# Grouped-query attention on one core: the first head's loads and turns in another order, the last head's output scaled and stored in another way

## The chip, the cores and the metric

The kernel runs on one core of a Trainium2 chip. The metric is device time in microseconds for one execution; lower is better. Each kernel was run several times, and the median is given with the lowest and the highest.

## The reference

```python
batch, n_q_heads, n_kv_heads, seq, head_dim = (8, 8, 2, 1024, 64)     # float32 q, k, v
...
scale = 1.0 / np.sqrt(head_dim)
for g in range(n_kv_heads):
    q_group, k_group, v_group = ...                                    # 4 q heads, 1 k head, 1 v head
    scores = scale * np.matmul(q_group, k_group.transpose(0, 1, 3, 2))
    attn = np.exp(scores - scores.max(-1))
    attn = attn / (attn.sum(-1) + 1e-08)
    output[:, heads of g] = np.matmul(attn, v_group)
```

There are 64 heads of q (8 batches of 8), each with 1024 queries and 1024 keys of length 64. Four heads of q share one head of k and v.

## The kernel before, in words

One head of q is a job; there are 64 jobs, j = 0 to 63. The scores of a job are computed transposed, keys on partitions: 8 pieces of 128 keys by 1024 queries. q and k lie in SBUF as bf16, transposed, with two rows of the sequence side by side, so that the 64 elements of the even rows lie on partitions 0 to 63 and those of the odd rows on 64 to 127. One score is a pair of matmuls (L735), one on each half of the partitions, into a PSUM tile of 128 x 1024 (two banks). There are three such tiles, sp0 to sp2, called slots.

A score is turned into exponentials in one of two ways. ScalarE (ACT) takes 382 of the 512 scores with its Exp function (L747). VectorE (DVE) takes the other 130 with an integer approximation: a pass out of PSUM (L758), then four passes in SBUF over two scores at once (L765, L772, L781, and L786 in the last two jobs). The results are the weights of the second product (L799), whose moving operand is v with a column of ones, so that the sum of the exponentials comes out as column 65. Its output goes to two more PSUM banks. VectorE takes reciprocals of the sums (L852), scales up to seven output pieces at a time into SBUF (L855), and SP stores a whole head (L870).

The order of the work on each engine is fixed when the kernel is built. A planner (class Plan) simulates PE, ACT and DVE with costs in nanoseconds and writes a list of events; M_START is the time at which it lets the first score start. Loads and casts are hung on this list at fixed distances before a job's first score: the cast of q to bf16 in DRAM 18 us before (POOL's queue, cast_q, L527), its transposing load 11 us before (SP's queue, turn_q, L570). Engines then wait for each other by semaphores alone.

The first job doesn't wait for that route. Its q and k are loaded as float32 (L589, L590): k's first chunk of 128 pairs of keys and then the other three on SP's queue, all of q on ACT's. While they are on their way, PE multiplies blanks (dummy, L600), eight of 512 columns. VectorE casts k's first chunk and q's second half to bf16 (L605, L607), ACT casts q's first half and the rest of k (L606, L608). PE turns the four chunks of q and then the four of k with an identity matrix (turn, L614): q into one slot, k's first chunk into another, the rest of k into the third. Then ACT copies columns 0 to 319 of the turned q to SBUF (L624), VectorE k's first chunk (L625), q's columns 320 to 511 (L626) and the rest of k (L627). The first score needs all of q and k's first chunk. Behind it PE computes k's other arrangement, even and odd rows swapped (swap_k0, L633), which VectorE copies (L637), and the remaining scores follow. The second score goes to VectorE, the third to ACT as its second exp. In gaps of this early stretch the planner puts more blanks of 128 columns.

The last job's second product is written to a free slot (L820), half of the eight output pieces in each bank, as soon as the last exps end. VectorE takes all eight reciprocals (L852), then scales the first four pieces (L855), and ACT the other four, one instruction each (L863). The two halves are stored separately (L831), the first on SP's queue and the second on ACT's. Each half is 128 partitions by two runs of 512 bytes; one partition's rows of the output lie 256 rows apart.

In what the traces print, q, k are tiles of the first job in float32 or bf16, qd and kd the casts in DRAM, qt and kt the transposed tiles, sp the slots, ops the two output banks, pt the results of ACT's exps, yt, zt and et VectorE's, and ost the ring of outputs in SBUF.

Of the kernel before, what the change touches and what calls it, by code (L numbers as in the profile page):

```python
# [8 lines left out]


M_START = 5800
M_SWAP = 1500
M_Q1 = 3400
M_QSTEP = 2700
# [11 lines left out]
M_FIX = 66  # L26
M_DTAIL = 80
M_DEP = 34
M_D1 = 1.042
# [18 lines left out]
PB = 7  # L48
NPIECE = 8
# [62 lines left out]
class Plan:  # L112
# [79 lines left out]
    def dve(self, s):  # L192
        t, nj, end = s.tD, self.nj, None
        if s.dq and s.dq[0][0] <= t:
            _, sl, j, c = s.dq.pop(0)
            n = len(STEPS) if j >= nj - TAIL else 3
            if s.open and s.open.nsteps != n:
                s.chains.append(s.open)
                s.open = None
            if s.open is None:  # L200
                s.open = Chain(s.nch, n)
                s.heads[s.nch] = []
                s.nch += 1
                s.used_c += 1
            ch = s.open
            ch.pairs.append((j, c))
            if j not in s.heads[ch.id]:
                s.heads[ch.id].append(j)
            self.gpsimd(s, t, j)
            s.note(t, "dpass", sl, (ch.id, len(ch.pairs) - 1), (j, c))  # L210
            end = t + M_FIX + 1024 * M_D1
            s.slot[sl] = end + M_DTAIL + M_SEE
            s.dlast = (ch.id, 0)
            if len(ch.pairs) == 2:
                s.chains.append(ch)
                s.open = None
        elif s.norms and s.norms[0][0] <= t and s.norms[0][1] == "rec":
            _, _, lo, hi = s.norms[0]
            s.note(t, "rec", (lo, hi), None, None)
            end = t + M_REC  # L220
            s.dlast = lo
            s.norms[0] = (end, "norm", lo, hi)
        else:
            best = None
            if s.norms and s.norms[0][0] <= t:
                late = s.dlast == s.norms[0][2]
                best = (late, 5 if late else 0, None)
# [224 lines left out]
def kernel(  # L452
# [158 lines left out]
    turned = {"k": new_slot(2)[:, 0, :], "q": new_slot(1)[:, 0, :], "k0": new_slot(0)[:, 0, :]}  # L611

    def turn(x, c):
        nc.tensor.matmul(  # L614
            turned["k0" if x == "k" and c == 0 else x][:, c * 128 : (c + 1) * 128],
            lhsT=b16[x][:, c, :], rhs=ident, start=True, stop=True,
        )

    for c in range(NH):
        turn("q", c)  # L620
    for c in range(NH):
        turn("k", c)
    QS = 320
    nc.scalar.activation(out=q0[:, 0, 0:QS], in_=turned["q"][:, 0:QS], func=AF.Copy)  # L624
    nc.vector.tensor_copy(out=k0[:, 0, 0:128], in_=turned["k0"][:, 0:128])  # L625
    nc.vector.tensor_copy(out=q0[:, 0, QS:HS], in_=turned["q"][:, QS:HS])  # L626
# [69 lines left out]
    for when, kind, x, j, c, *cols in ev:  # L696
# [30 lines left out]
        elif kind == "score":  # L727
# [4 lines left out]
            for half in range(2):  # L732
# [7 lines left out]
                    stop=True,  # L740
                )
            if len(where_s) == 1:
                swap_k0()
        elif kind == "act":
            p = pp.tile([128, 2, HS], BF16, name="pt")
# [81 lines left out]
                    )  # L827
        elif kind == "half":
            b, h = divmod(NJ - 1, H)
            r = plan.last % RING + x * 4  # L830
            (nc.scalar if x else nc.sync).dma_start(  # L831
                out=rows(out[b, h])[:, 2 * x : 2 * x + 2],
                in_=ost[:, r : r + 4, :].rearrange("p (s two) d -> p s (two d)", two=2),
            )
        elif kind in ("rec", "norm"):
            lo, hi = x
# [2 lines left out]
            if lo < plan.last:  # L839
                o = ops[plan.group_of[lo] % 2][:, 0 : n * (D + 1)]  # L840
                o = o.rearrange("p (s d) -> p s d", d=D + 1)
                sums = o[:, :, D]
            else:
                o2 = sps[plan.spare][:, :, 0 : 4 * (D + 1)]
                o2 = o2.rearrange("p b (s d) -> p b s d", d=D + 1)
                o, sums = o2[:, 0], o2[:, :, :, D]
            if kind == "rec":
                rec = rp.tile([128, NPIECE], FP32, name="rec")
                to = rec[:, 0:n]
                if lo >= plan.last:  # L850
                    to = to.rearrange("p (b s) -> p b s", b=2)
                vec = nc.vector.reciprocal(out=to, in_=sums)  # L852
            else:
                n = min(n, PB if lo < plan.last else 4)
                vec = nc.vector.tensor_tensor(  # L855
                    out=ost[:, r : r + n, :],
                    in0=o[:, :, 0:D],
                    in1=rec[:, 0:n].unsqueeze(2).to_broadcast([128, n, D]),
                    op=ALU.mult,
                )  # L860
                if lo >= plan.last:
                    for i in range(4):
                        nc.scalar.activation(  # L863
                            out=ost[:, r + 4 + i, :], in_=o2[:, 1, i, 0:D],
                            func=AF.Copy, scale=rec[:, 4 + i : 5 + i],
                        )
        elif kind == "store":
            b, h = divmod(j, H)
            r = j * NPIECE % RING
# [35 lines left out]
```

The softmax here doesn't subtract the row's maximum and nothing guards it: scores larger than these inputs give would overflow.

## Time and profile before

| | |
|---|---|
| Median of 5 runs | 364.87 us (364.27 to 365.48) |
| The profiled execution's own time | 364.27 us |
| Its span, first to last instruction | 362.5 us |
| Busy: PE, DVE, ACT, POOL | 96%, 97%, 98%, 14% |
| First score, first exp | 6.13 us, 6.56 us |
| End of the last second product, last store issued | 357.5 us, 359.27 us |

PE is TensorE's matmul row, PEld its weight loads, which overlap matmuls. DVE is VectorE, ACT is ScalarE, POOL is GpSimd, SP the engine that only issues DMAs; a q behind a name (SPq) stands for an engine's sequencer, which waits and issues. A number behind L is a line of the kernel. Times of a timeline or chain are microseconds from the span's start: the start, then the duration.

### The profile page before, as it was taken

What the parts mean: (1) busy time and instruction counts of PE and PEld (TensorE: products, weight loads), DVE (VectorE), ACT (ScalarE), POOL (GpSimd) and SP (SyncE); (2) the same over time, 40 slices, a digit from 0 to 9 for tenths busy, and PEclk for the clock granted to TensorE, in tenths of its full rate; (3) what the DMA queues carried; (4) which work ended last, traced back from release to release, by engine and by line L of the source; (5) the groups of instructions that cost most, each with busy time, mean ns of one, the idle gap of its engine ahead of it and who ended that gap; (6) DMA issues with size and microseconds to landing.
All of it is one profiled execution on the core that took longest, in us unless ns stands there. A gap on an engine that the chain in (4) does not pass through costs nothing.

```text
span 362.5 us, 13853 instructions
## 1 busy us (share of the span) xinstructions
PE 347.2 (96%) x6179; PEld 222.1 (61%) x6179; DVE 350.2 (97%) x481; ACT 354.1 (98%) x390; POOL 50.8 (14%) x100
## 2 busy tenths in 40 slices
PE   8879999999999999999999999999999999999993
PEld 3436666666666666666666666666666666656563
DVE  4999999999999999999999999999999999999992
ACT  5999999999999999999999999999999999999995
POOL 3121111111111111110111211111112101110000
PEclk9999999999999999999999999999999999999999
DMA  6635789377766874696576687768668776763223
GB/s 158 119 72 98 140 136 175 74 156 138 123 129 111 166 137 97 138 141 140 75 145 136 132 147 117 150 132 148 115 119 128 153 132 105 160 134 62 60 60 89
DMA packets 89307, 44.81 MB, mean 124 GB/s; under 512 B 45504, under 2 KB 87616, under 8 KB 88000
## 3 DMA queue, kind: packets, MB, share of 16 engines
q1 hardware_dynamic: 86336, 33.31, 41.3%
q0 software_dynamic: 2496, 10.23, 22.8%
q8 instruction: 48, 0.79, 0.9%
q10 hardware_dynamic: 416, 0.39, 0.4%
q14 instruction: 11, 0.09, 0.1%
HBM read 25.17 MB, written 27.00 MB: 144 GB/s over the span
## 4 chain that ended last, share of the span: by engine, by line
ACT 95%; PE 3%; issue 1%; DVE 0%
ACT pt L747 95%; PE ops L600 1%; PE sp L820 1%; PE sp L735 0%; PE ops L799 0%; ACT ost L863 0%; ACT qt L624 0%; PE sp L614 0%; DVE qt L626 0%; DVE warm L519 0%
## 5 line engine op out<-in xcount | busy, mean ns | idle before, releaser
L747 ACT ACTIVATE pt<-sp 128x1024 bf16<-128x1024 f32 x382 | 350.5, 1067 | 0.9 <-PE sp L735 0.9
L735 PE MATMUL sp<-qt,kt 64*128 64x512 bf16 x1024 | 173.9, 382 | 8.6 <-ACT pt L747 4.7
L799 PE MATMUL ops<-va,pt 128*128 128x65 bf16 x3008 | 181.7, 194 | 0.0
L799 PEld LDWEIGHTS <-pt 128*128 128x128 bf16 x3008 | 139.8, 98 | 34.1 <-issue 34.1
L758 DVE TENSOR_SCALAR yt<-sp 128x1024 uint16<-128x1024 f32 x130 | 158.1, 1216 | 0.3 <-PE sp L735 0.2
L799 PE MATMUL ops<-va,zt 128*128 128x65 bf16 x1024 | 136.0, 194 | 0.0
L799 PE MATMUL ops<-va,et 128*128 128x65 bf16 x1008 | 133.0, 195 | 0.0
L799 PEld LDWEIGHTS <-et 128*128 128x128 bf16 x1008 | 85.7, 98 | 30.4 <-issue 29.8
L799 PEld LDWEIGHTS <-zt 128*128 128x128 bf16 x1024 | 88.4, 98 | 7.5 <-issue 7.5
L735 PEld LDWEIGHTS <-kt 64*128 64x128 bf16 x1024 | 48.1, 93 | 57.1 <-issue 35.2
L781 DVE TENSOR_TENSOR zt<-yt,zt 128x2048 bf16<-128x2048 bf16 x65 | 78.2, 1204 | 0.0
L527 POOL DMA_DIRECT2D qd<-in_q_dram x63 | 32.5, 516 | 187.8 <-PE sp L735 176.7
L855 DVE TENSOR_TENSOR ost<-ops,rec 128x448 f32<-128x448 f32 x72 | 44.2, 614 | 0.0
L765 DVE TENSOR_SCALAR zt<-yt 128x2048 uint16<-128x2048 uint16 x65 | 44.0, 677 | 0.2
L772 DVE TENSOR_SCALAR et<-yt 128x2048 uint16<-128x2048 uint16 x65 | 43.3, 666 | 0.0
L535 POOL DMA_DIRECT2D kd<-in_k_dram x15 | 7.9, 525 | 51.5 <-PE sp L735 51.5
L552 POOL CAST va<-vs 128x512 bf16<-128x512 f32 x16 | 9.9, 617 | 36.6 <-DVE zt L781 16.4
L852 DVE RECIPROCAL rec<-ops 128x7 f32<-128x7 f32 x72 | 14.1, 196 | 0.0
L600 PE MATMUL ops<-warm 128*128 128x128 bf16 (+1 forms) x35 | 6.1, 315 | 1.2 <-DVE warm L519 1.2
L600 PEld LDWEIGHTS <-warm 128*128 128x128 bf16 x35 | 2.6, 108 | 4.6 <-issue 3.4
L852 DVE RECIPROCAL rec<-sp 128x8 f32<-128x8 f32 x1 | 0.2, 208 | 2.4 <-PE sp L820 2.4
L605 DVE CAST k<-k 128x128 bf16<-128x128 f32 x1 | 0.2, 228 | 2.3 <-DMA k<-in_k_dram 2.3
(30 smaller groups left out, 17.7 us busy)
## 6 DMA issues: line engine op xcount, KB each, us to landing
out_dram<-ost SPq DMA_DIRECT2D x63, 256.0 KB, 3.3
qd<-in_q_dram POOLq DMA_DIRECT2D x63, 128.0 KB, 3.6
vs<-in_v_dram SPq DMA_DIRECT2D x16, 256.0 KB, 4.1
kd<-in_k_dram POOLq DMA_DIRECT2D x15, 128.0 KB, 3.2
kt<-kt SPq DMA_DIRECT2D x30, 64.0 KB, 2.9
qt<-qd SPq DMA_TRANSPOSE x63, 4.3
q<-in_q_dram ACTq DMA_DIRECT2D x1, 256.0 KB, 3.1
kt<-kd SPq DMA_TRANSPOSE x15, 4.3
```

What stands on the lines that cost most here:

```text
L527: return nc.gpsimd.dma_start(out=t.rearrange("(a x) d -> a (x d)", x=4), in_=q[b, h].rearrange("(a x) d -> a (x d)", x=8),)
L552: return nc.gpsimd.tensor_copy(out=va[:, b * G + g, :, :, 0:D], in_=vs.pop((b, g)).rearrange("p c (two d) -> p c two d", two=2),)
L600: nc.tensor.matmul(ops[1][:, 0:cols], lhsT=warm[:, 0:128], rhs=warm[:, 0:cols], start=True, stop=True)
L735: now = nc.tensor.matmul(sps[x][:, half, :], lhsT=t[lo : lo + D, c // NH, ci % NH * 128 : (ci % NH + 1) * 128], rhs=qt[j][lo : lo + D, 0, ...
L747: exps.append(nc.scalar.activation(out=p, in_=where_s[(j, c)], func=AF.Exp, scale=scale))
L758: vec = nc.vector.tensor_scalar(out=yt[ch][:, i, :, :], in0=where_s[c], scalar1=EXP_A, scalar2=EXP_B, op0=ALU.mult, op1=ALU.add,)
L765: vec = nc.vector.tensor_scalar(out=zt[j][:, 0:c], in0=yt[j][:, 0:c], scalar1=0x7F, scalar2=0x3F00, op0=ALU.bitwise_and, op1=ALU.bitwise_or,)
L772: vec = ins = nc.vector.tensor_scalar(out=et[j][:, 0:c], in0=yt[j][:, 0:c], scalar1=0x7F80, scalar2=None, op0=ALU.bitwise_and,)
L781: vec = nc.vector.tensor_tensor(out=z, in0=flat(yt[j])[:, 0:c, 0 : cols[0]], in1=z, op=ALU.mult)
L799: nc.tensor.matmul(ops[plan.group_of[x] % 2][:, lo : lo + D + 1], lhsT=p[:, qs * 128 : (qs + 1) * 128], rhs=va[:, b * G + h // HPG, ci % N ...
L852: vec = nc.vector.reciprocal(out=to, in_=sums)
L855: vec = nc.vector.tensor_tensor(out=ost[:, r : r + n, :], in0=o[:, :, 0:D], in1=rec[:, 0:n].unsqueeze(2).to_broadcast([128, n, D]), op=ALU ...
```

## The change

It has two places. At the start, the loads are split in four: k's first chunk and q's chunks 2 and 3 on ACT's queue, q's chunks 0 and 1 and the rest of k on SP's. There are six blanks of 512 columns and three of 128. The turned q goes into two slots: chunks 0 and 1 into one that only ACT reads, chunks 2 and 3 into another, beside k's first chunk, that only VectorE reads. The rest of k is cast by ACT after its copy of q, turned by PE after the first score, and then copied by VectorE (rest_k0). M_START is 5400 instead of 5800.

At the end, VectorE scales all eight pieces in one instruction, and ACT none. Each half of the store now takes 64 partitions, with 2 KB that lie together in DRAM for each partition. For that, the last job's q is cast with its rows in another order (cast_q), in 512 pieces of 256 bytes written. The planner's cost of the last scaling changes accordingly.

```diff
-M_START = 5800
+M_START = 5400
...
-                    end = at + M_FIX + 64 * min(hi - lo, PB if lo < self.last else 4) * M_D1
+                    end = at + M_FIX + 64 * (hi - lo) * M_D1
...
+        if j == NJ - 1:
+            return nc.gpsimd.dma_start(
+                out=t.rearrange("(c p) d -> p c d", p=128), in_=rows(q[b, h], True)
+            )
...
-    for c, n in ((0, 1), (1, NH - 1)):
-        nc.sync.dma_start(out=f32["k"][:, c : c + n], in_=rows(k[0, 0], True)[:, c : c + n])
-    nc.scalar.dma_start(out=f32["q"], in_=rows(q[0, 0], True))
+    for e, x, lo, hi in (
+        (nc.scalar, "k", 0, 1), (nc.sync, "q", 0, 2), (nc.scalar, "q", 2, NH), (nc.sync, "k", 1, NH)
+    ):
+        src = {"q": q, "k": k}[x][0, 0]
+        e.dma_start(out=f32[x][:, lo:hi], in_=rows(src, True)[:, lo:hi])
...
-    dummy(8, HS)
-    nc.vector.tensor_copy(out=b16["k"][:, 0:1], in_=f32["k"][:, 0:1])
-    ins = nc.scalar.activation(out=b16["q"][:, 0:2], in_=f32["q"][:, 0:2], func=AF.Copy)
-    nc.vector.tensor_copy(out=b16["q"][:, 2:NH], in_=f32["q"][:, 2:NH])
-    nc.scalar.activation(out=b16["k"][:, 1:NH], in_=f32["k"][:, 1:NH], func=AF.Copy)
+    dummy(6, HS)
+    dummy(3, 128)
+    place(nc.vector, "k", 0, 1)
+    ins = place(nc.scalar, "q", 0, 2)
+    place(nc.vector, "q", 2, NH)
...
-    for c in range(NH):
-        turn("q", c)
-    for c in range(NH):
-        turn("k", c)
-    QS = 320
-    nc.scalar.activation(out=q0[:, 0, 0:QS], in_=turned["q"][:, 0:QS], func=AF.Copy)
-    nc.vector.tensor_copy(out=k0[:, 0, 0:128], in_=turned["k0"][:, 0:128])
-    nc.vector.tensor_copy(out=q0[:, 0, QS:HS], in_=turned["q"][:, QS:HS])
-    nc.vector.tensor_copy(out=k0[:, 0, 128:HS], in_=turned["k"][:, 128:HS])
+    turn("q", 0, 2, s1[:, 0])
+    turn("q", 2, NH, s0[:, 1])
+    turn("k", 0, 1, s0[:, 0])
+    h = HS // 2
+    nc.scalar.activation(out=q0[:, 0, 0:h], in_=s1[:, 0, 0:h], func=AF.Copy)
+    nc.vector.tensor_copy(out=q0[:, 0, h:HS], in_=s0[:, 1, h:HS])
+    nc.vector.tensor_copy(out=k0[:, 0, 0:128], in_=s0[:, 0, 0:128])
+    place(nc.scalar, "k", 1, NH)
+
+    def rest_k0():
+        turn("k", 1, NH, s2[:, 0])
+        nc.vector.tensor_copy(out=k0[:, 0, 128:HS], in_=s2[:, 0, 128:HS])
...
             if len(where_s) == 1:
+                rest_k0()
                 swap_k0()
...
-            r = plan.last % RING + x * 4
+            r = plan.last % RING
+            lo = x * 64
             (nc.scalar if x else nc.sync).dma_start(
-                out=rows(out[b, h])[:, 2 * x : 2 * x + 2],
-                in_=ost[:, r : r + 4, :].rearrange("p (s two) d -> p s (two d)", two=2),
+                out=rows(out[b, h], True)[lo : lo + 64],
+                in_=ost[lo : lo + 64, r : r + NPIECE, :].rearrange(
+                    "p (s two) d -> p s (two d)", two=2
+                ),
             )
...
-                n = min(n, PB if lo < plan.last else 4)
-                vec = nc.vector.tensor_tensor(
-                    out=ost[:, r : r + n, :],
-                    in0=o[:, :, 0:D],
-                    in1=rec[:, 0:n].unsqueeze(2).to_broadcast([128, n, D]),
-                    op=ALU.mult,
-                )
-                if lo >= plan.last:
-                    for i in range(4):
-                        nc.scalar.activation(
-                            out=ost[:, r + 4 + i, :], in_=o2[:, 1, i, 0:D],
-                            func=AF.Copy, scale=rec[:, 4 + i : 5 + i],
-                        )
+                to, by = ost[:, r : r + n, :], rec[:, 0:n].unsqueeze(2).to_broadcast([128, n, D])
+                if lo < plan.last:
+                    o = o[:, :, 0:D]
+                else:
+                    o = o2[:, :, :, 0:D]
+                    to = to.rearrange("p (b s) d -> p b s d", b=2)
+                    by = by.rearrange("p (b s) d -> p b s d", b=2)
+                vec = nc.vector.tensor_tensor(out=to, in0=o, in1=by, op=ALU.mult)
```

More of the change, by code (lines that the diff above doesn't have):

```diff
@@ L602, in dummy @@
             )
-    dummy(8, HS)
-    nc.vector.tensor_copy(out=b16["k"][:, 0:1], in_=f32["k"][:, 0:1])
-    ins = nc.scalar.activation(out=b16["q"][:, 0:2], in_=f32["q"][:, 0:2], func=AF.Copy)
-    nc.vector.tensor_copy(out=b16["q"][:, 2:NH], in_=f32["q"][:, 2:NH])
-    nc.scalar.activation(out=b16["k"][:, 1:NH], in_=f32["k"][:, 1:NH], func=AF.Copy)
-    tc.add_manual_dep(load_v(0, 0).ins, ins.ins.name, Sync, reason="loads in time, not sooner")
-    turned = {"k": new_slot(2)[:, 0, :], "q": new_slot(1)[:, 0, :], "k0": new_slot(0)[:, 0, :]}
@@ L613, in turn @@
[L613 to L616, printed above, removed]
-        )
-    for c in range(NH):
-        turn("q", c)
-    for c in range(NH):
-        turn("k", c)
-    QS = 320
-    nc.scalar.activation(out=q0[:, 0, 0:QS], in_=turned["q"][:, 0:QS], func=AF.Copy)
-    nc.vector.tensor_copy(out=k0[:, 0, 0:128], in_=turned["k0"][:, 0:128])
-    nc.vector.tensor_copy(out=q0[:, 0, QS:HS], in_=turned["q"][:, QS:HS])
@@ L627, with place @@
-    nc.vector.tensor_copy(out=k0[:, 0, 128:HS], in_=turned["k"][:, 128:HS])
+    dummy(6, HS)
+    dummy(3, 128)
+    def place(e, x, lo, hi):
+        to, src = b16[x][:, lo:hi], f32[x][:, lo:hi]
+        if e is nc.vector:
+            return e.tensor_copy(out=to, in_=src)
+        return e.activation(out=to, in_=src, func=AF.Copy)
+    place(nc.vector, "k", 0, 1)
+    ins = place(nc.scalar, "q", 0, 2)
+    place(nc.vector, "q", 2, NH)
+    tc.add_manual_dep(load_v(0, 0).ins, ins.ins.name, Sync, reason="loads in time, not sooner")
@@ new lines, with turn @@
+    s0, s1, s2 = new_slot(0), new_slot(1), new_slot(2)
+    def turn(x, lo, hi, to):
+        for c in range(lo, hi):
+            nc.tensor.matmul(
+                to[:, c * 128 : (c + 1) * 128], lhsT=b16[x][:, c, :], rhs=ident,
+                start=True, stop=True,
+            )
+    turn("q", 0, 2, s1[:, 0])
[4 more added lines that the diff above has]
+    nc.vector.tensor_copy(out=q0[:, 0, h:HS], in_=s0[:, 1, h:HS])
@@ L845 @@
                 o2 = o2.rearrange("p b (s d) -> p b s d", d=D + 1)
-                o, sums = o2[:, 0], o2[:, :, :, D]
+                sums = o2[:, :, :, D]
             if kind == "rec":
@@ L853 @@
             else:
-                n = min(n, PB if lo < plan.last else 4)
-                vec = nc.vector.tensor_tensor(
-                    out=ost[:, r : r + n, :],
-                    in0=o[:, :, 0:D],
-                    in1=rec[:, 0:n].unsqueeze(2).to_broadcast([128, n, D]),
-                    op=ALU.mult,
-                )
-                if lo >= plan.last:
-                    for i in range(4):
-                        nc.scalar.activation(
-                            out=ost[:, r + 4 + i, :], in_=o2[:, 1, i, 0:D],
-                            func=AF.Copy, scale=rec[:, 4 + i : 5 + i],
-                        )
+                to, by = ost[:, r : r + n, :], rec[:, 0:n].unsqueeze(2).to_broadcast([128, n, D])
[6 more added lines that the diff above has]
+                vec = nc.vector.tensor_tensor(out=to, in0=o, in1=by, op=ALU.mult)
         elif kind == "store":
```

## The prediction, made before the changed kernel was run

> **What bounds the kernel now.** I read the page first (busy shares, the chain that ended last), then the chain in order of time, then the timelines of the first 9 and the last 6 us. The page's chain by engine, and its costliest groups:
>
> ```profile
> ACT 95%; PE 3%; issue 1%; DVE 0%
> ...
> L747 ACT ACTIVATE pt<-sp 128x1024 bf16<-128x1024 f32 x382 | 350.5, 1067 | 0.9 <-PE sp L735 0.9
> ```
>
> 382 exps on ScalarE fill 95% of the span and wait once, for the first score. The chain in order of time (start, duration, what) shows what stands before and behind them:
>
> ```profile
> 1.19 3.60 PE ops L600 x8
> 4.79 0.44 PE sp L614 x4
> 5.23 0.02 issue
> 5.25 0.45 ACT qt L624
> 5.70 0.02 issue
> 5.72 0.37 DVE qt L626
> 6.09 0.04 issue
> 6.13 0.41 PE sp L735 x2
> 6.54 0.02 issue
> 6.56 24.69 ACT pt L747 x27
> ...
> 355.27 2.28 PE sp L820 x64
> 357.54 0.77 issue
> 358.32 0.13 ACT ost L863
> ```
>
> Everything the change touches on this chain lies before 6.56 us or after 357.5. In the middle, 27 exps take 24.69 us (0.914 each), and VectorE is as full: 60.00 busy of 60.00 us between 60 and 120 us. So neither engine has slack to absorb a late start, and what the start gains or loses reaches the end. The timeline (start, duration, engine, line, [idle before <- releaser]) of the two places that matter:
>
> ```profile
> 6.91 0.69 DVE L637 CAST kt<-ops 128x512 bf16<-128x512 f32 x1 [0.37 <-PE ops L633]
> 8.98 1.22 DVE L758 TENSOR_SCALAR yt<-sp 128x1024 uint16<-128x1024 f32 x1 [0.25 <-PE sp L735]
> ...
> 357.81 0.42 DVE L855 TENSOR_TENSOR ost<-sp,rec 128x256 f32<-128x256 f32 x1
> 358.26 0.37 SPq L831 DMA_DIRECT2D out_dram<-ost  x1
> 358.32 0.93 ACT L863 ACTIVATE ost<-sp,rec 128x64 f32<-128x64 f32 x4 [1.27 <-PE sp L820]
> 359.27 0.40 ACTq L831 DMA_DIRECT2D out_dram<-ost  x1
> ```
>
> VectorE's last idle moment is the 0.25 us before 8.98; that pass waits for a score whose PSUM slot exp 2 frees. So exp 2, more than exp 1, sets the pace of both engines. Exp 1 starts at 6.561, exp 2 at 7.481, exp 3 at 8.385: exp 2 was 0.016 us later than the 0.904 rhythm, because its score was done at 7.426. The score path behind exp 1 has no slack.
>
> [...] DVE L626 starts at 5.72, when ACT L624 (5.25 + 0.44) has finished with the same tile, and ACT L863 starts at 358.32, behind DVE's 357.81 + 0.42, though the reciprocal that it needs was done at 357.78. [...] Here the clock record turns full at 5.84 us; blanks before it are 0.427 us apart, turns 0.107, and score pairs after it 0.227. [...]
>
> **The start.** Before: q (256 KB) lands at 3.84, k's first chunk at 4.01, the rest of k at 4.29. After, four loads go out: k chunk 0 then q 2:4 on ACT's queue, q 0:2 then the rest of k on SP's. The second issue costs ACT 0.42 us ahead of its table load (1.28), which then ends near 2.95, under the loads. In before's packet records some 430 KB had gone out by 3.35 us. In the new order q 2:4 is through at about that amount; with the 0.40 us that q took from last packet to landing, it lands at X = 3.75. Earlier than 3.5 the bytes ahead of it exclude; by 4.1 nearly all has landed. q 0:2 I put at 3.5.
>
> Blank matmuls: six of 512 columns and three of 128 from 1.19: 6 x 0.427 + 3 x 0.107 = 2.88, so PE is free at 4.07 instead of 4.58. Half of q is cast by ACT (0.42) at 3.94 and turned at 4.1; ACT copies it by about 4.95, beside the following.
>
> The path that decides runs through VectorE: cast of q 2:4 (wait 0.02, 0.286), 0.056 to PE, two q turns and the k turn at 0.107 spacing, so the k turn starts X + 0.58 and ends 0.314 later. VectorE's copy of q's half waits for that k turn, since both lie in one PSUM tile (its wait counts past it): starts X + 0.93. Its length is 0.42 (0.357 for 192 columns, 0.293 for 128); the k0 copy follows 0.342 later and takes 0.293, 0.056 to PE: first score at T = X + 1.62 = 5.37 (before 6.13), exp 1 at T + 0.43 = 5.80 instead of 6.56. That 0.76 is not what reaches the end.
>
> Exp 2 needs the rest of k0, whose turning is moved behind the first score. From T: 0.32 until PE can issue after a score pair (as 6.132 to 6.455), three turns at 0.056, the last done at T + 0.66, VectorE's copy of 384 columns 0.70 to 1.256 (0.548), PE at T + 1.31; the swap matmuls fit in between. Then the pair for VectorE, and 0.227 later the one for exp 2, 0.376 long, 0.075 to ACT: exp 2 at T + 1.99 = 7.36, against 7.48. ACT idles about 0.66 us after exp 1. The cast of k's rest, moved behind ACT's q copy, ends near 5.5, before PE asks for it (5.69); uncovered it would cost at most its 0.52. VectorE's first pass starts at T + 1.75 = 7.12 instead of 7.52, then waits for exp 2's slot as before. **Start: -0.12**; with X from 3.5 to 4.1, from -0.37 to +0.23.
>
> **The middle: nothing.** The planner's start goes from 5800 to 5400, but the instructions stand in the same order on every engine from the first scores on, apart from a few 128-column blanks (two fewer, three more) in PE gaps. The last q's cast becomes 512 pieces instead of 16 long ones. It was issued at 326.62 and landed 2.9 us later; SP's transpose behind it issued at 329.96, 11 us before its use by the plan, and the next store in SP's queue only at 335.61. So 5 us more stay hidden. A gain is excluded. [...] VectorE's SBUF passes took 0.677 us with and without a POOL issue beside them: zero, at most 0.5. The v load waits for ACT's first cast and moves with it; the three transposes behind it on SP wait for the casts as before (5.70), so POOL and SP stay as they are.
>
> **The tail.** Removed: ACT's four scalings (0.93) and the 0.09 ahead of them. Added: 256 more columns on VectorE. From 614 ns for 448 columns (L855) and 0.42 for 256, 512 take 0.68: done at 358.49, both issues at 358.52 instead of 358.26 and 359.27. Alone, a half store began moving 0.87 to 0.92 us after issue and landed after 1.82 to 1.85. Now both move together: 128 pieces of 2 KB at 84 ns (the q load's) on 16 engines are 0.67, with ramp 0.75, and 0.35 to the landing: 358.52 + 0.90 + 0.75 + 0.35 = 360.52 against 361.13. **Tail: -0.61.** If they don't disturb each other -0.78; if one waits for the other's issue, -0.25.
>
> **Sum.** -0.12 - 0.61 = -0.73 against the profiled execution: 362.5 to 361.8 of span, 364.27 to 363.54 of its own time. The median of the five runs lies 0.60 above that execution, so 364.87 becomes 364.14; I take 364.1. A measurement of this kernel tells about 0.2% (0.73 us) from no change, so the forecast lies just at that edge.
>
> **Rivals.** (1) The start gives nothing or takes: X = 4.0, so exp 2 comes at 7.61 (+0.13), and the stores half serialize (-0.45): 364.55, no change. For it: q 2:4 stands second in a queue, and before, the second load of a queue landed at 4.29. Against it: it has 128 KB, not 192. (2) All of exp 1's lead reaches the end: -0.76 - 0.61, 363.5. For it: ACT is 95% of the chain. Against: exp 2's score path above. (3) Slower: [...] Before, the stretch 2.43 to 5.84 had 3.21 us of PE work out of 3.41; after, I count about 2.6 (blanks to 4.07, turns, then a gap until the first score). [...] From T on it then issues six pairs, eight swaps and some 16 blanks, 1.36 + 0.22 + 0.90 = 2.48, at twice the time; some goes into gaps, and I take +1.5 for the start: 364.87 + 1.5 - 0.6 = 365.8. It decides from +1.34. [...] (4) The change doesn't do what it says: the waits of the built program show ACT and VectorE reading different tiles, so this is out for the q copies.
>
> **How the numbers follow.** Forecast 0.50, rival 1 0.31, rival 2 0.06, rival 3 0.13. The first and third are faster (0.55, a little of them falling short), rival 1 the same (0.32), the last slower (0.13). The range 363.5 to 364.9 holds all but rival 3 and a few per cent. The likeliest case's own range is 363.6 to 364.4.
>
> **What would show it.** First exp near 5.8, a gap of about 0.6 after it, exp 2 near 7.4, then the 0.904 rhythm; the wait before exp 2 put down to PE's score. Clock full no later than before. One L855-like pass of 128x512 near 0.68 us at the end, no scaling on ACT, both stores issued within 0.05 us and landing 2.0 us later. Wrong if exp 2 comes after 7.5, if a store takes over 2.3 us to land, or if an exp in the middle waits where none did.

## The result: 0.4% slower, and the profile after

The changed kernel takes 366.14 us in the median of 25 runs (364.42 to 368.94); the kernel before, timed beside it, 364.99 (364.08 to 366.49, 46 runs). The ratio is 1.0038, with a 95% interval of 1.0027 to 1.0049. (Runs of both kernels fall into groups, so this ratio, like those below, lies nearer to that of the means than to that of the medians.) The forecast was 364.1, with a range up to 364.9.

The profiled execution of the changed kernel is the slowest of its 25 runs, 368.94 us. It shows every loss at once, and two of them have to be kept apart below. First the page: the clock row, the chain by engine, and the two groups that wait for scores (busy and mean of one, then idle before them and its releaser).

```profile
PEclk9997999999999999999999999999999999999998
...
ACT 91%; PE 5%; DMA 1%; issue 1%; DVE 1%; ACTq 0%
...
L765 ACT ACTIVATE pt<-sp 128x1024 bf16<-128x1024 f32 x382 | 351.3, 1066 | 4.9 <-PE sp L752 4.8
...
L776 DVE TENSOR_SCALAR yt<-sp 128x1024 uint16<-128x1024 f32 x130 | 158.1, 1216 | 3.5 <-PE sp L752 3.2
```

The exps cost what they cost before (1066 ns against 1067), but ScalarE now waits 4.9 us for scores instead of 0.9, and VectorE waits with it. The 7 in the clock row, the slice from 27.5 to 36.7 us of the span, is the mark of a spell at half TensorE clock; the trace's clock record has it from 26.07 to 32.90, after 13.65 us at full clock. In this profile and in those of e1, e2, e7 and e8, which have such spells too, the changes lie multiples of 3.41 us apart; that length is called a clock step below, a window in the recorded expectations. The chain in order of time (start, duration, what) gives the start:

```profile
1.16 3.23 DMA q<-in_q_dram
4.41 0.30 DVE q L615
4.76 0.51 PE sp L628 x3
5.30 0.42 DVE qt L638
5.72 0.21 DVE kt L639
5.98 0.61 PE sp L752
6.58 0.45 PE sp L628 x3
7.06 0.57 DVE kt L644
7.67 1.04 PE sp L752 x4
8.71 0.64 PE ops L605 x5
9.36 0.54 PE sp L752 x2
```

In the kernel before, the chain was with ScalarE from 6.56 us on. Here it stays with PE and VectorE until 12.61. The timeline of the same place (start, duration, engine, line, [idle before <- releaser]) shows ScalarE's side:

```profile
5.98 0.61 PE L752 MATMUL sp<-qt,kt 64*128 64x512 bf16 x2 [0.72 <-DVE kt L639]
6.63 1.02 ACT L765 ACTIVATE pt<-sp 128x1024 bf16<-128x1024 f32 x1 [1.33 <-PE sp L752]
7.06 0.56 DVE L644 CAST kt<-sp 128x384 bf16<-128x384 f32 x1 [1.14 <-PE sp L628]
8.32 1.23 DVE L776 TENSOR_SCALAR yt<-sp 128x1024 uint16<-128x1024 f32 x1
8.75 1.02 ACT L765 ACTIVATE pt<-sp 128x1024 bf16<-128x1024 f32 x1 [1.10 <-PE sp L752]
```

Exp 1 starts at 6.63 (before: 6.56), exp 2 at 8.75 (7.48), exps 3 to 5 at 9.94, 11.44 and 12.61, when before had 8.38, 9.29 and 10.19. The score pair at 5.98 takes 0.61 us; the first pair of before took 0.39. That is the half clock, as in the spell that the record shows, where the pair at 26.52 takes 0.61 as well: the trace's clock record turns full at 12.42 here, and at 5.84 before. (The page's clock row says nothing about the time ahead of the first record; one reads it from such durations.)

The end, from the timeline, and the landing line of the two stores:

```profile
362.08 0.21 DVE L873 RECIPROCAL rec<-sp 128x8 f32<-128x8 f32 x1 [2.42 <-PE sp L838]
362.32 0.69 DVE L882 TENSOR_TENSOR ost<-sp,rec 128x512 f32<-128x512 f32 x1
363.04 0.52 SPq L850 DMA_DIRECT2D out_dram<-ost  x1
363.04 0.56 ACTq L850 DMA_DIRECT2D out_dram<-ost  x1
```

```profile
DMA to landing us min/median/max: 2.4/2.5/2.7
```

From the start of the reciprocal to the last landing it is 362.08 to 365.71, 3.63 us; before it was 357.57 to 361.13, 3.56. The end was to bring 0.61 and brings nothing.

Add up how far the starts of successive exps lie apart beyond the regular 0.904 us. Up to 13 us into the span this excess is 2.38 us (before 0.01), from 13 to 40 us 2.42 (before 0.42), afterwards 4.56 (before 4.48). With 0.07 for exp 1 and 0.07 for the end the differences make 4.59 of the 4.67 us between the two profiled executions. So there are three questions: the first 13 us, the stretch from 13 to 40, and the end.

### The profile page after: what moved, and what is told of

It reads as the page before. It is cut to its first block, busy times and chain, and to the rows that moved or that the text cites. A ratio compares the mean times of both kernels' runs of the same rounds, so it can differ in the third digit from the quotient of the medians.

```text
span 367.2 us, 13851 instructions
## 1 busy us (share of the span) xinstructions
PE 351.8 (96%) x6181; PEld 223.4 (61%) x6181; DVE 351.1 (96%) x481; ACT 353.8 (96%) x386; POOL 51.0 (14%) x100
## 4 chain that ended last, share of the span: by engine, by line
ACT 91%; PE 5%; DMA 1%; issue 1%; DVE 1%; ACTq 0%
ACT pt L765 91%; PE sp L752 2%; PE ops L817 1%; DMA q<-in_q_dram 1%; PE sp L838 1%; PE ops L605 0%; PE sp L628 0%; DVE ost L882 0%; DVE kt L644 0%; DVE qt L638 0%; ACTq L595 0%; DVE q L615 0%; DVE rec L873 0%; DVE kt L639 0%
## 5 line engine op out<-in xcount | busy, mean ns | idle before, releaser
L765 ACT ACTIVATE pt<-sp 128x1024 bf16<-128x1024 f32 x382 | 351.3, 1066 | 4.9 <-PE sp L752 4.8
L752 PE MATMUL sp<-qt,kt 64*128 64x512 bf16 x1024 | 176.4, 388 | 8.3 <-ACT pt L765 4.5
```

Of the source, the lines that this page charges most:

```text
L752: now = nc.tensor.matmul(sps[x][:, half, :], lhsT=t[lo : lo + D, c // NH, ci % NH * 128 : (ci % NH + 1) * 128], rhs=qt[j][lo : lo + D, 0, ...
L765: exps.append(nc.scalar.activation(out=p, in_=where_s[(j, c)], func=AF.Exp, scale=scale))
```

## The experiments

With this profile the theory was: the loss lies in the start, because PE's clock opens late, and that is so because PE has too little to do (rival 3 of the prediction). Its rival: the order of the work behind the first score is what costs, at any clock.

**Which half of the change.** e2_tail_only is the kernel before with the changed end (cast_q, "half", "norm" and the planner's line); e3_start_only is the changed kernel with the end of before, all of that part of the diff reversed:

```diff
 e2_tail_only, against before
+        if j == NJ - 1:
+            return nc.gpsimd.dma_start(
+                out=t.rearrange("(c p) d -> p c d", p=128), in_=rows(q[b, h], True)
+            )
...
+            lo = x * 64
...
-                if lo >= plan.last:
-                    for i in range(4):
-                        nc.scalar.activation(
...
```

> The kernel before with the end of the change alone: one scaling on VectorE, both halves by partitions in 2 KB pieces, the last q cast in other rows. The prediction's tail: 0.6 us faster, 364.4. Stores-in-each-other's-way theory (in the changed kernel's trace the second half begins to move 1.8 us after its issue, not 0.9): 0.0 to 0.2 us faster, with the last landing 3.5 to 3.7 us after the last reciprocal starts, as before.

> The changed kernel with the end of before: the four scalings on ACT and the stores by runs of 512 bytes. If the end gives nothing, as its trace says, 366.0 to 366.3, like the changed kernel. If the end gives the predicted 0.6 us and the start loses more than it shows, 366.7.

Measured: e2_tail_only 364.80 us (364.02 to 366.27, 14 runs), ratio 1.0004 [0.9989, 1.0019]. e3_start_only 366.30 (366.25 to 366.39, 6 runs), 1.0042 [1.0027, 1.0058]. The start alone makes the whole loss. The end alone shows no gain: in e2's profile the last landing comes 3.66 us after the reciprocal's start, as late as in the changed kernel. e3's profile is the plain case, without the spell at 27 us: ScalarE's timeline has

```profile
6.60 1.02 ACT L762 ACTIVATE pt<-sp 128x1024 bf16<-128x1024 f32 x1 [1.30 <-PE sp L749]
8.72 1.02 ACT L762 ACTIVATE pt<-sp 128x1024 bf16<-128x1024 f32 x1 [1.10 <-PE sp L749]
```

with the clock full from 10.19 us, an excess of 1.65 up to 13 us and 0.41 from 13 to 40. Here the wait ahead of exp 2 and what follows it until the clock opens is all there is, and it makes 1.64 of the loss.

**Is it the fewer blanks?** e4_before_fewer is the kernel before with the changed kernel's blanks. e1_fill gives the changed kernel twelve more, around the last turns before the first score:

```diff
 e4_before_fewer, against before
-    dummy(8, HS)
+    dummy(6, HS)
+    dummy(3, 128)
 e1_fill, against after
     turn("q", 0, 2, s1[:, 0])
+    dummy(4, 128)
...
     turn("k", 0, 1, s0[:, 0])
+    dummy(8, 128)
```

> The kernel before with six blanks of 512 columns and three of 128 in place of eight of 512, nothing else. PE is then idle from 4.07 us until q's cast at 4.33. Clock theory: [...] 365.0 to 366.0 with single ones above 366.5. Order theory: PE reaches the q turn 0.25 us earlier and nothing else changes, 364.7 to 365.0.

> The changed kernel with 12 more blank matmuls of 128 columns: four between q's second and third turn, eight behind the k turn, where PE stood idle for 0.5 and 0.9 us before its first score. Clock theory [...]: [...] the exps keep their 0.904 us rhythm from the third on, and the median falls from 366.1 to 365.0 or below. Order theory (turning the rest of k behind the first score costs the time whatever the clock does): the blanks change nothing, 366.0 to 366.3.

Measured: e4_before_fewer 365.17 (363.81 to 367.30, 22 runs), 1.0001 [0.9987, 1.0014]. In its profile the clock is full at 4.02, the first score comes at 5.65 and the exps at 6.08, 7.00, 7.90, without a stall. e1_fill 365.96 (364.58 to 367.29, 22 runs), 1.0031 [1.0019, 1.0043].

To read these two, one needs the clock share that each run's record gives. It leaves out the time ahead of the run's first clock record (before's profiled execution has 0.998, though its clock is full only from 5.84), so it doesn't show a late opening; one clock step of 3.41 us at half clock later on takes 0.005 from it, and 0.996 or more means that no whole clock step was lost after the opening. Among the 153 runs of before beside the experiments, all those with 0.996 or more took at most 364.35 us.

On average, fewer blanks alone cost nothing in e4. But six of its 22 runs lie at 365.37 to 365.76 with a share of 0.997, a place where before has none, and its median and its one run at 367.30 are what the clock theory expected. It is likely that the clock opened late in these six; none of them was profiled. So fewer blanks, the cause behind rival 3, probably act in some executions, and they don't explain by themselves why most runs of the changed kernel lose.

In e1 the clock theory's median is missed, but its other sign came: the exps keep the rhythm from the second on (6.75, 8.38, 9.30, 10.21), with the clock full at 6.88 in the profile. That execution took 367.20 because of what came later: its excess is 0.74 up to 13 us, but 2.21 from 13 to 40, with the clock at half from 23.95 to 30.78. Of e1's nine runs with a share of 0.996 or more, eight lie at 364.58 to 365.18; of the changed kernel's ten, eight lie at 365.79 to 366.25. So the blanks do make the start shorter, and a second loss hides it in the median. The gap that stays in e1 is the one behind the first score.

**Loads or order?** e7_after_loads is the changed kernel with the loads of before. e8_after_order is the changed kernel, all four loads and slots included, but with the rest of k cast, turned and copied ahead of the first score, where before had it:

```diff
 e7_after_loads, against after
-    for e, x, lo, hi in (
-        (nc.scalar, "k", 0, 1), (nc.sync, "q", 0, 2), (nc.scalar, "q", 2, NH), (nc.sync, "k", 1, NH)
-    ):
...
+    for c, n in ((0, 1), (1, NH - 1)):
+        nc.sync.dma_start(out=f32["k"][:, c : c + n], in_=rows(k[0, 0], True)[:, c : c + n])
+    nc.scalar.dma_start(out=f32["q"], in_=rows(q[0, 0], True))
 e8_after_order, against after
     place(nc.vector, "q", 2, NH)
+    place(nc.scalar, "k", 1, NH)
...
     turn("k", 0, 1, s0[:, 0])
+    turn("k", 1, NH, s2[:, 0])
...
     nc.vector.tensor_copy(out=k0[:, 0, 0:128], in_=s0[:, 0, 0:128])
-    place(nc.scalar, "k", 1, NH)
-    def rest_k0():
...
+    nc.vector.tensor_copy(out=k0[:, 0, 128:HS], in_=s2[:, 0, 128:HS])
...
-                rest_k0()
```

> The changed kernel with the loads of before (k's two parts on SP's queue, all of q on ACT's). In the changed kernel's trace q's second half lands at 4.39 us, 0.64 later than predicted, and the first score follows it. Here all of q should land near 3.84, the first score start near 5.5, and at full clock the second exp near 7.5. If the late landing is the main loss, directly and by PE's gap that it leaves, the median is 364.5 to 365.2; if it is the rest of k behind the first score, 365.8 to 366.3.

> The changed kernel, but the rest of k cast, turned and copied before the first score, as in the kernel before. The first score stays near 6.0 us. If the chain of turn, copy and scores between the first and the second exp is the loss, the second exp follows the first within 1.1 us even at half clock and the median falls to 364.8 to 365.4. If the late second load and the clock make the loss by themselves, 365.8 to 366.3.

Measured: e7_after_loads 365.81 (364.41 to 367.66, 22 runs), 1.0028 [1.0016, 1.0041]. e8_after_order 364.43 (364.02 to 366.23, 14 runs), 0.9995 [0.9980, 1.0010]. The loads hardly matter; the place of the rest of k does. e7's profile happens to have an open clock at the start, full from 5.01 us (its time, 366.00 us, holds a spell at half clock from 25.49 to 28.90). Its ScalarE timeline:

```profile
6.16 1.02 ACT L763 ACTIVATE pt<-sp 128x1024 bf16<-128x1024 f32 x1 [0.64 <-PE sp L750]
7.70 1.94 ACT L763 ACTIVATE pt<-sp 128x1024 bf16<-128x1024 f32 x2 [0.51 <-PE sp L750]
```

At full clock exp 2 still comes 1.54 us after exp 1, 0.64 more than the rhythm, and then it runs on. In e8's profiled execution, its slowest at 366.23 us because the clock is at half from 23.24 to 30.07, the clock opens later (6.17), and still the first four exps follow one another without idle time:

```profile
6.31 3.77 ACT L762 ACTIVATE pt<-sp 128x1024 bf16<-128x1024 f32 x4 [1.05 <-PE sp L750]
```

So the moved work is a stall of its own at any clock, and the old order has none even behind a first score at half clock. What the changed order leaves between exps 1 and 2 is a chain: three turns, VectorE's copy, and two score pairs. Four of e8's 14 runs lie at 365.57 to 365.81 with a share of 0.996 or more; e8 has e4's fewer blanks, and like e4's six these runs were not profiled.

**Filling PE.** e5_before_hole is the kernel before with 31 blanks of 128 columns between the scores at 19.5 to 26 us, where PE has no second product to do. They go to columns of an output bank that nothing uses then; the other instructions keep their order. e6_after_hole gives the changed kernel the same blanks. e12_after_filled has these, e1's twelve, and three more behind swap_k0:

```diff
 e5_before_hole and e6_after_hole, against before and after
+    pes = sorted((e for e in plan.ev if e[1] in ("score", "pv", "dummy")), key=lambda e: e[0])
+    held = {}
+    since = max(e[0] for e in pes if e[1] == "pv" and e[2] < NPIECE)
+    until = min(e[0] for e in pes if e[1] == "pv" and e[2] >= NPIECE)
+    for a, b in zip(pes, pes[1:]):
+        if a[1] == "score" and since < a[0] < until:
+            held[(a[3], a[4])] = max(0, min(6, int((b[0] - a[0] - M_PAIR - 100) / 60)))
...
+            if held.get((j, c)):
+                dummy(held[(j, c)], 128, 384)
 e12_after_filled, against e6, beside the two lines of e1
         nc.vector.tensor_copy(out=k0[:, 1, :], in_=ops[0])
+        dummy(3, 128)
```

> The kernel before with 31 more blanks of 128 columns behind the scores of 19.5 to 26 us, where PE does nothing but scores while it waits for the second job's weights (its array streams 39% of the time there); they write columns of the output bank that are not yet in use. Clock theory: the clock no longer falls to half for a window or two between 23 and 31 us, which is what parts the runs of before into a group at 364.2 and one at 365.3; nearly all runs then lie at 364.2 to 364.4 and so does the median. If the two groups come from something else, both stay and the median is 364.8 to 365.2.

> The changed kernel with the same 31 blanks at 19.5 to 26 us. Clock theory: the runs above 366.6 vanish, the main group at 366.0 to 366.3 stays, since it is the late opening at the start that makes it, median 366.0. Order theory: the same, so it tells only how much of the loss lies in the fall of the clock; if the main group itself moves to 365 or below, the loss was not at the start.

> The changed kernel with e1's twelve blanks, three more behind the swap matmuls, where PE waits for VectorE's copy of k, and e6's 31 blanks, so that the fall after 23 us is out. What is left is the opening. If PE's gaps before and after the first score are what keeps the clock down (e6: 15 of 22 runs over 365.4), at most a third of the runs stays over 365.4 and the median is 364.5 to 365.0. If it opens late with these gaps filled too, most runs stay over 365.4 and the median is 365.7 to 366.1.

Measured: e5_before_hole 364.25 (363.79 to 364.66, 22 runs), 0.9975 [0.9965, 0.9985], faster than both kernels. e6_after_hole 365.77 (364.33 to 366.35, 22 runs), 1.0013 [1.0000, 1.0025]. e12_after_filled 365.00 (364.50 to 365.35, 13 runs), 1.0004 [0.9995, 1.0012].

The 46 runs of before beside the changed kernel fall into two groups, 19 at 364.08 to 364.34 and the rest at 364.87 and above. With the blanks at 20 us only the lower group is left. The clock shares say the same of the 153 runs named above: 0.996 or more in every run up to 364.35, 0.986 to 0.994 in every run from 364.85 on. The table by stretches shows where the clock is lost: PE's busy time, then weight loads, VectorE, ScalarE and GpSimd, granted clock, share of DMA and GB/s. The changed kernel:

```profile
20.00:24.00 4.00, 3.14 (x44) 1.67 (x42) 4.00 (x6) 4.00 (x6) 0.49 (x1) 1.00 0.54 98
24.00:28.00 4.00, 2.86 (x15) 0.62 (x13) 4.00 (x6) 4.00 (x5) 1.20 (x2) 0.76 0.15 33
28.00:34.00 6.00, 6.00 (x85) 3.99 (x84) 4.08 (x6) 4.27 (x6) 0.75 (x2) 0.59 0.19 25
```

The kernel before, in the execution that was profiled:

```profile
20.00:24.00 4.00, 2.10 (x14) 0.59 (x12) 4.00 (x6) 4.00 (x6) 0.62 (x1) 1.00 0.26 66
28.00:34.00 6.00, 5.98 (x112) 3.97 (x111) 6.00 (x9) 6.00 (x7) 1.18 (x2) 1.00 0.57 101
```

And e5_before_hole:

```profile
20.00:24.00 4.00, 3.85 (x37) 2.16 (x36) 4.00 (x5) 4.00 (x5) 0.62 (x1) 1.00 0.29 68
28.00:34.00 6.00, 5.99 (x108) 3.76 (x104) 6.00 (x8) 6.00 (x8) 1.20 (x2) 1.00 0.61 111
```

Both kernels leave PE half empty for some four microseconds around 20 to 27 us. In the changed kernel's profile PE is busy for 2.03 of the 3.41 us up to 26.07, and the clock is at half from there to 32.90: between 28 and 34 us only 85 matmuls get through instead of 112, and ScalarE is busy for 4.27 of 6.00 us. In the profiled execution of before the clock held, with PE busy for 2.06 of the 3.42 us from 19.49 to 22.91; in e2's, with the same order there, it was half from 23.99 to 27.40 and the excess from 13 to 40 us was 1.23. It is a loss that the kernel before has too. In e6 the blanks take away the runs above 366.4 (5 of 25 without them, none of 22 with them), but the median stays at 365.77, and its exps 1 and 2, at 6.83 and 8.95, lie 2.12 us apart as in the changed kernel.

e12 then shows the share of the clock in the rest. With the gaps before and behind the first score filled, no run is above 365.4, where e6 had 15 of 22. Its clock is full at 6.25, and ScalarE's timeline is e7's again:

```profile
6.54 1.02 ACT L777 ACTIVATE pt<-sp 128x1024 bf16<-128x1024 f32 x1 [1.24 <-PE sp L762]
8.06 1.94 ACT L777 ACTIVATE pt<-sp 128x1024 bf16<-128x1024 f32 x2 [0.51 <-PE sp L762]
```

So 365.77 to 365.00 is what filling those gaps gives back; in the two profiles the clock is full at 10.01 in e6 and at 6.25 in e12, and the excess up to 13 us falls from 1.52 to 0.64. From there to e5's 364.25 it is 0.75 us. The 0.64 is the stall of the order, which the blanks leave as it is, and the changed end, which e5 doesn't have, adds the 0.07 from above.

**The late second load.** q's second half landed at 4.39, not 3.75. e11_cast_later issues the cast of job 1's q after the identity matrix is made. In the changed kernel's trace the casts' packets (8 KB, 624 ns each in the median) start at 3.46, beside those of q's second half (2.62 to 3.97):

```diff
 e11_cast_later, against after
-    cast_q(1)
     make_identity(nc, ident)
+    cast_q(1)
     cast_q(2)
```

> The changed kernel with the first cast of the next q issued on POOL's queue after the identity is made, about 0.9 us later, so that its 8 KB packets (624 ns each) don't stand among those of q's second half. If they are what holds q's second half back, it lands at 3.8 to 3.95 us instead of 4.39, and the first score starts at 5.5. If the second issue on a queue is late by itself, it lands at 4.3 to 4.5 as before. The median tells little: 365.5 to 366.2 in either case.

Measured: 366.53 (366.06 to 367.21, 4 runs), 1.0044 [1.0028, 1.0059]. The load landed at 4.09 in its profile, the clock was full at 10.47, exps 1 and 2 came at 6.34 and 8.46. In the other profiles with these loads the same transfer landed between 3.98 and 4.58, so a single 4.09 settles nothing; the cause stays open. An earlier first score gained nothing here in any case: exp 2 still came 2.12 us after exp 1.

**The end.** e9_best takes e5 with e4's blanks and changes only the scaling at the end: VectorE scales the second half in a second instruction, and the two stores stay as they were before. e10_one_store takes e5 with the changed end, but as one store of 128 partitions by 2 KB on SP's queue:

```diff
 e9_best, the end, against before
                 if lo >= plan.last:
-                    for i in range(4):
-                        nc.scalar.activation(
...
+                    vec = nc.vector.tensor_tensor(
+                        out=ost[:, r + 4 : r + 8, :],
+                        in0=o2[:, 1][:, :, 0:D],
+                        in1=rec[:, 4:8].unsqueeze(2).to_broadcast([128, 4, D]),
+                        op=ALU.mult,
+                    )
 e10_one_store, the end, against after
-            lo = x * 64
-            (nc.scalar if x else nc.sync).dma_start(
-                out=rows(out[b, h], True)[lo : lo + 64],
...
+            if x:
+                continue
+            lo = 0
+            nc.sync.dma_start(
+                out=rows(out[b, h], True)[lo : lo + 128],
...
```

> The kernel before with the 31 blanks of e5 at 19.5 to 26 us, six blanks of 512 and three of 128 at the start, and the last second half scaled by VectorE too, in a second instruction, with the stores of before. The second store is then issued some 0.65 us sooner than before, 0.4 us behind the first. If stores that start 0.4 us apart don't hold each other up, the last landing comes 3.0 us after the last reciprocal starts (before 3.56) and the median is 363.6 to 363.8; with e4's fewer blanks worth up to 0.3 in addition, 363.3. If they do hold each other up as in the changed kernel, 3.5 us and 364.0 to 364.3.

> e5 (the kernel before with the 31 blanks) with the changed end, but one store of 128 partitions by 2 KB on SP's queue in place of two of 64 on two queues. If it is the second queue's store waiting for the first that took the gain, one issue of 0.37 us, 0.9 us to the first packet and 0.7 us of packets at 84 ns bring the last landing 3.0 us after the last reciprocal starts, and the median goes from e5's 364.25 to 363.7. If 2 KB pieces out of SBUF are slow themselves (155 ns each in the changed kernel's first half), the packets take 1.2 us, the landing comes after 3.5 us, and 364.2 stays.

Measured: e9_best 363.35 (363.15 to 365.24, 22 runs), 0.9971 [0.9959, 0.9983]. e10_one_store 363.68 (363.48 to 363.79, 5 runs), 0.9963 [0.9950, 0.9976]. e9's end in the timeline:

```profile
357.31 0.42 DVE L865 TENSOR_TENSOR ost<-sp,rec 128x256 f32<-128x256 f32 x1
357.65 0.41 DVE L872 TENSOR_TENSOR ost<-sp,rec 128x256 f32<-128x256 f32 x1
357.76 0.37 SPq L841 DMA_DIRECT2D out_dram<-ost  x1
358.09 0.40 ACTq L841 DMA_DIRECT2D out_dram<-ost  x1
```

and e10's, with its landing:

```profile
357.81 0.69 DVE L878 TENSOR_TENSOR ost<-sp,rec 128x512 f32<-128x512 f32 x1
358.52 0.34 SPq L846 DMA_DIRECT2D out_dram<-ost  x1
```

```profile
DMA to landing us min/median/max: 2.0/2.0/2.0
```

From the reciprocal's start to the last landing e9 takes 2.96 us (357.07 to 360.03) and e10 2.97 (357.56 to 360.53), against 3.56 before and 3.63 after. Both gain the 0.6 that the changed end doesn't. One store of the same 2 KB pieces lands after 2.0 us; two halves of it issued at the same moment on two queues land after 2.4 and 2.7. In the changed kernel the issues themselves take 0.52 and 0.56 instead of 0.37 and 0.40, the first packets move 1.17 us (SP) and 1.78 us (ACT) after issue, and SP's packets take 155 ns each where e10's take 85 to 88. So the loss lies in the two stores as the changed end issues them, and not in 2 KB pieces: 0.33 us between two issues (e9), or a single one (e10), go without it. What in them costs isn't settled, since e9's halves have 128 partitions and 512-byte runs, and two stores of 64 partitions some time apart were not tried. The shared moment is the nearest reason, but it isn't enough for the long issues: the first loads of both kernels are issued within 0.01 us of each other on the same two queues too, and their issues take 0.39 to 0.42. Why SP's packets are slow is not shown either.

## Why the prediction was wrong, step by step

**q lands at X = 3.75: wrong.** It was 4.39, outside the 3.5 to 4.1 that the prediction allowed, and 3.98 to 4.58 over the profiles with these loads. The failed sentence is "In the new order q 2:4 is through at about that amount": the estimate by bytes put the landing 0.64 us too early, and what held it until 4.39 is not shown. Rival 1 had X = 4.0.

**First score at X + 1.62: right.** 5.98 - 4.39 = 1.59. Exp 1 then comes 0.65 after the score instead of 0.43, since the pair runs at half clock (0.61 us instead of 0.39). That exp 1 isn't what counts was right as well: it starts 0.07 us later than before, and the median is 1.15 us higher.

**Exp 2 at T + 1.99 (T is the start of the first score), with 0.66 us of idle time: the mechanism was right, its size was read at the wrong clock.** With an open clock it is exact: in e7 exp 2 comes at 7.70 for a T of 5.73, T + 1.97. In the changed kernel it is 8.75 for 5.98, T + 2.77. The term that failed took every step from T on at full-clock durations (turns at 0.056, pairs 0.227 apart and 0.376 long), though the prediction has the clock of before turn full only at 5.84 us, and T was put at 5.37. At half clock the pairs are 0.40 apart and 0.63 long, and the following pairs hold up exps 3 to 5. The sum then balanced a stall of 0.66 against an exp 1 that was to be 0.76 earlier; with X late, there was nothing to set against the stall.

**Clock "no later than before": wrong, and it is about half of the loss or more.** Filling the gaps gave back 0.77 of the 1.52 us between e6 and e5; in e3's execution the excess is 1.65 where the order costs 0.64 at full clock. Counted back from 12.42 in clock steps of 3.41 us, PE was busy in the changed kernel for 2.79 us from 2.18 to 5.59, for 2.94 in the next and for all of the third, at whose end the clock turned full. Before, it was busy for 3.21 of the 3.41 us up to 5.84. How busy PE must be for that is not shown. Rival 3 had this outcome: 365.8 against a measured 366.14, by work at half clock behind the first score. The clock was full 4.35 us later than before in e3's execution (10.19) and 6.58 later in the page's (12.42). But it was given 0.13, and its cause, fewer blanks, is a part at most: with them alone (e4) six of 22 runs look like a late opening, while in e6 15 of 22 lie above 365.4. The changed kernel with the eight wide blanks of before was not tried, so how large that part is stays open. The other empty places are the waits for q's late half and for VectorE's copies, ahead of and behind the first score. They go together with the clock: the serial chain behind the first score leaves PE idle, the clock is full at 10.01 with those gaps (e6) and at 6.25 with them filled (e12), and at half clock the pairs of the chain are 0.40 us apart instead of 0.227. e8 undoes the order and e12 fills the gaps, and each takes its part away.

**The middle, "nothing": right about the moved instructions, wrong about the time.** No run points to the last q's cast in 512 pieces, and VectorE's pass of 512 columns took 0.69 as worked out (0.68). But the working looked at waits and queues and not at PE's empty stretch at 20 to 27 us, where the clock fell in six of the profiled executions, three with the old order of the start and three with the new; their excess from 13 to 40 us is 1.23 to 2.43, against 0.42 in the kernel before. The profile of before showed that stretch as 2.10 us of PE work in 4.00, and nothing in it said that the clock was near to falling.

**The tail, -0.61: wrong, +0.07.** Every step up to the issue was right (issue 0.96 after the reciprocal's start, as worked out). The term that failed is the 2.0 us to the landing, "with ramp 0.75": it was 2.36 and 2.67. The bound "if one waits for the other's issue, -0.25" wasn't low enough either. As a single store it is -0.6 (e10), so the estimate was right for a transfer that the change does not issue. (Its 84 ns is the median of the q load's packets, whose mean was 126; e10's packets took 86 on average.) Issuing the two at once saved nothing either: the issues took 0.52 and 0.56 us, a single one 0.34 (e10).

**The sum.** Forecast -0.12 - 0.61. In e3's execution the first term is +1.68 by the end of the exps; the second is +0.07 in the changed kernel's. The largest group of the changed kernel's runs (17 of 25 at 365.8 to 366.3) is not one case: by their clock shares, 8 are like e3's execution, late at the start and without a later fall (0.996 or 0.997), and 9 lost about one clock step of 3.41 us to half clock after the opening (0.994), as e7's execution at 366.00 did. The prediction's own three signs of being wrong came about in the changed kernel's profile: exp 2 after 7.5, both stores over 2.3 us from issue to landing, and exps in the middle that wait.

## What to carry to other kernels

Work that is moved behind the first result isn't free because it is no longer in front: price the chain from the first result to the second, at the clock that holds there, and check that the engine that waits has something to do meanwhile. When PE's durations decide, look for stretches in which it idles, in the middle of the kernel too; 31 short blanks in such a place (PE busy for 3.85 instead of 2.10 us between 20 and 24) made the kernel before 0.25% faster and its times even. When several groups of times stand side by side, compare runs with the same clock share before a median is read. Two halves of a last store, issued at the same moment, brought nothing here; one store, or two of another form 0.33 us apart, brought 0.6 us.

## What the runs showed of the hardware that was not expected

- The clock fell at 26.07 in the changed kernel's profile after 3.41 us in which PE was busy for 2.03, though the trace has it idle for no more than 0.52 us at a time there. In the kernel before it was busy for 2.06 of the 3.42 us from 19.49 to 22.91, and the clock stayed full. Counted in columns of the matmul records (some of which may be missing), at the 0.427 us of a blank of 512 at half clock and half of that at full, the array streams 38% of the first stretch and 39% of the second. So neither count tells by itself when the clock falls.
- The clock steps lie at another phase in each execution: counted back, the changes at 5.84 (before), 12.42 (the changed kernel), 10.19 (e3) and 5.01 (e7) fall at 2.43, 2.18, 3.36 and 1.60. The times of one kernel fall into groups 1.1 to 1.9 us apart; that the phase over PE's empty stretches makes the groups is the author's estimate. e9 keeps such a second group (8 of 22 runs at 364.65 to 365.24) in spite of the blanks at 20 us. Its clock shares there are 0.997 and 0.998, so nothing fell after the opening; e5, which has the eight wide blanks, has no run above 364.66. A late start with fewer blanks, as in e4, is the likely reason; no such run was profiled.
- Two stores of 64 partitions issued 4 ns apart on SP's and ACT's queues were both slow: first packets 1.17 and 1.78 us after issue, against 0.87 to 0.92 for the two of before, issued 1.01 us apart.
- The best versions here are e9_best (median 363.35) and e10_one_store (363.68, all runs within 0.31 us). e8's order with e5's blanks and e10's store was not tried.
